# Out projection, way up and way down of a two-block transformer on one core: buffers laid over freed bytes, and the order of work at the borders of the stages

## The chip, the core and the metric

The kernel runs on one core of a Trainium2 chip. The core has TensorE (matmuls and transposes into PSUM; PE in the profile, its weight loads PEld), VectorE (DVE), ScalarE (ACT), GpSimd (POOL) and SyncE (SP), which here issues every transfer, one after the other. The metric is device time in microseconds; lower is better. The times are whole executions; the profile is one further execution.

## What is computed

Two transformer blocks over 1024 rows of 1024 float32 numbers, one after the other. Cut to the parts around the change:

```python
# first block
x = x + mix @ w_out                       # mix: attention, conv and pool branches
h2 = rms_norm(x, norm2_g)
up = causal_depthwise_conv(h2 @ w_up, ffn_dw_w)      # 5632 columns, width 3
gate, val = split(up)
x = x + (silu(gate) * val) @ w_down       # 2816 rows
# second block
h = rmsnorm(x, pre_mix_w)                 # feeds q, k, v and the gates
x = x + rmsnorm(merged @ w_out, post_mix_w)
h = rmsnorm(x, pre_ffn_w)
f = (silu(h @ w_gate) * (h @ w_up)) @ w_down
x = x + rmsnorm(f, post_ffn_w)
```

## The kernel before

Every float32 operand of a matmul is split into a high part (a cast on ScalarE) and a low part (raw minus high, on GpSimd or VectorE in turn, `lo_of`), and a product of two operands is three matmuls (`mm3`, L117): high by high, high by low, low by high. A matmul has 128 x 128 weights and mostly 512 columns.

The stages run one after the other: `mix1` (norm, projections, attention and branches), `out1` (first out projection), `ffn` with the convolution, then a norm and transposes, `mix2`, `merge2`, `out2` (second out projection, then its norm and the sum with x), and `ffn` without convolution, which ends with the last norm. `ffn` has three parts.

- `ffn_prelude` normalises the eight row blocks of 128 rows (Square on ScalarE, L734; the inverse root on GpSimd, L155 and L157; the scaling on VectorE, L736), forms sums and differences of their quarters, and transposes seven operands T1 to T7 of 512 x 512 (`put`, L719 to L726: four transposes, a cast on ScalarE, the low part on VectorE). T1 and T2 come from rows 0 to 3 as they are; the other five need rows 4 to 7 as well.
- `ffn_up` multiplies by a scheme of seven products in place of eight (of the kind of Strassen's). For each of 22 channel blocks it loads two weight tiles, forms four sums, splits them (`split`, L778) and runs seven products of 12 matmuls, 84 in all. Partial results are copied from PSUM (`snap`, L837), summed into G and V (`add`, L850), sent through convolution and SiLU (`finish`, L809), and the operands of the way down go to DRAM (gD).
- `ffn_down` runs 11 pairs of channel blocks in groups of 2, 3, 3 and 3: it loads operands from gD and from w_down (`load`, L890), splits them (L931, L932), runs seven products per group and adds them to the accumulator rows `acc` (`to`, L905; L912), which in the first block are loaded from x1D first (L888).

On each engine a scheduler of the tile framework fixes the order of the instructions at build time; the code's order and the tiles' lifetimes steer it. A tile that takes bytes of an earlier one waits for that one's last reader. Transfers stand in one queue on SyncE: one that waits holds up those behind it. `ffn` opens its pools when the stage before has closed its own:

```python
            with self.pool("fpre") as fp:
                self.ffn_prelude(rows, keep, g, T, fp, ps)
            close_rows()
            with self.pool("fst", side="right") as st:
                self.ffn_up(T, fw, st, ps, Wg, cg, Wu, cu, conv, gD)
```

## Time and profile before

| what | value |
|---|---|
| time, median of 3 runs | 2932.63 us (2928.97 to 2937.85) |
| the profiled execution, its time | 2919.26 us |
| its span | 2917.4 us |
| mean granted clock of TensorE in it | 0.963 |
| TensorE busy | 2711.6 us |
| VectorE, ScalarE, GpSimd busy | 1802.7, 1210.0, 909.9 us |
| transfers | 375.10 MB, 129 GB/s on average |

Busy is time in which an engine has an instruction in work. A count of matmuls in a stretch, beside the count in a stretch of the same matmuls without waits, tells how much of the stretch was lost; a waits view tells which engine's result ended each wait. A few records can be missing, so a count is good to about one per cent.

### The profile page before, as it was taken

To read this page: it belongs to the slowest core of one execution; us is meant where nothing else is said; L and a number is where in the kernel's file an instruction comes from. 1 tells how busy PE (TensorE), PEld (TensorE's weight loads), DVE (VectorE), ACT (ScalarE), POOL (GpSimd) and SP (SyncE) were. 2 spreads that over 40 slices of the span, in tenths; PEclk is the share of its full clock that TensorE was granted. 3 is DMA by queue.
4 is the path that set the end of the run, shared out by engine and by line. 5 is a ranking of instruction groups with operands and counts; after the bars stand their busy time and mean duration, and the time that the engine had idled before them with its cause. 6 is when DMAs were issued, how large, how long until landed. Compare 5 with 4: busy or idle time off the path is not lost. (4 is left out here: it accounts for less than half of the span.)

```text
span 2917.4 us, 37487 instructions
## 1 busy us (share of the span) xinstructions
PE 2711.6 (93%) x13686; PEld 2269.2 (78%) x13686; DVE 1802.7 (62%) x2832; ACT 1210.0 (41%) x1951; POOL 909.9 (31%) x686
## 2 busy tenths in 40 slices
PE   7999889699999889989999999999986999998997
PEld 7799678477777767878889988887875888886776
DVE  4697653678788796735666533444436555556877
ACT  4344561344444433334445444444313433334333
POOL 3256331122222244521211254323511212123445
PEclk9999999699999989989999999999996999999999
DMA  5444451122322383065664395415430333336532
GB/s 175 122 136 127 144 177 67 52 80 98 109 94 87 130 312 129 26 204 161 173 171 121 111 224 131 138 60 182 137 130 15 100 102 101 102 106 230 169 122 87
DMA packets 318145, 375.10 MB, mean 129 GB/s; under 512 B 42692, under 2 KB 215168, under 8 KB 317448
## 3 DMA queue, kind: packets, MB, share of 16 engines
q1 hardware_dynamic: 317960, 372.70, 41.2%
q8 instruction: 108, 1.77, 0.2%
q14 instruction: 77, 0.63, 0.1%
HBM read 257.01 MB, written 115.61 MB: 128 GB/s over the span
## 5 line engine op out<-in xcount | busy, mean ns | idle before, releaser
L138 POOL TENSOR_TENSOR wl<-wr,wh 128x1024 fp32r<-128x1024 f32 x73 | 184.8, 2534 | 343.4 <-ACT wh L137 303.8
L759 POOL TENSOR_TENSOR lo<-x,hi 128x1024 fp32r<-128x1024 f32 x77 | 205.7, 2684 | 270.5 <-ACT hi L931 269.1
L931 ACT CAST hi<-x 128x1024 fp32r<-128x1024 f32 x154 | 153.1, 1052 | 274.1 <-PE x L117 123.4
L759 POOL TENSOR_TENSOR wl<-ws,wh 128x512 fp32r<-128x512 f32 x88 | 115.6, 1315 | 469.8 <-ACT wh L781 383.5
L117 PE MATMUL mm<-hTh,wh 128*128 128x512 f32 x608 | 244.2, 402 | 4.1 <-ACT gs L1125 4.1
L117 PE MATMUL mm<-hTh,wl 128*128 128x512 f32 x608 | 241.6, 397 | 0.0
L309 ACT ACTIVATE t<-t,mx 128x640 f32<-128x640 f32 (+3 forms) x192 | 173.3, 903 | 163.4 <-DVE mx L305 154.6
L117 PE MATMUL mm<-hTl,wh 128*128 128x512 f32 x608 | 241.1, 396 | 0.0
L117 PE MATMUL mm<-wh,hTh 128*128 128x256 f32 (+1 forms) x752 | 228.9, 305 | 3.8 <-ACT hTh L184 1.9
L117 PE MATMUL mm<-wh,hTl 128*128 128x256 f32 (+1 forms) x752 | 228.4, 304 | 1.4 <-DVE hTl L185 1.4
L117 PE MATMUL mm<-wl,hTh 128*128 128x256 f32 (+1 forms) x752 | 227.9, 303 | 0.3 <-POOL wl L138 0.3
L781 ACT CAST wh<-ws 128x512 fp32r<-128x512 f32 x176 | 109.2, 623 | 263.1 <-PE x L117 145.0
L357 DVE TENSOR_TENSOR pl<-tr,ph 128x512 fp32r<-128x512 f32 (+2 forms) x160 | 100.6, 633 | 126.2 <-ACT ph L356 48.6
L326 POOL TENSOR_SCALAR t<-t,rs 128x640 f32<-128x640 f32 (+7 forms) x128 | 106.7, 840 | 204.3 <-DVE rs L325 179.8
L117 PE MATMUL x<-hi 128*128 128x512 f32 x352 | 139.7, 405 | 31.4 <-DVE f L912 17.1
L759 POOL TENSOR_TENSOR wl<-wr,wh 128x1024 fp32r<-128x1024 f32 (+1 forms) x44 | 94.0, 2136 | 200.5 <-ACT wh L781 160.1
L117 PEld LDWEIGHTS mm<-wh,hTh 128*128 128x128 f32 x752 | 144.9, 193 | 11.6 <-ACT hTh L184 2.9
L117 PEld LDWEIGHTS mm<-wh,hTl 128*128 128x128 f32 x752 | 145.0, 193 | 7.1 <-DVE hTl L185 1.6
L117 PEld LDWEIGHTS mm<-wl,hTh 128*128 128x128 f32 x752 | 145.1, 193 | 6.3 <-POOL wl L138 0.9
L117 PE MATMUL x<-lo,hi 128*128 128x512 f32 x352 | 140.6, 400 | 4.2 <-DVE lo L759 2.9
L117 PE MATMUL x<-hi,lo 128*128 128x512 f32 x352 | 140.1, 398 | 0.0
L117 PEld LDWEIGHTS mm<-hTh,wh 128*128 128x128 f32 x608 | 116.2, 191 | 29.2 <-ACT gs L1125 5.2
(334 smaller groups left out, 7764.6 us busy)
## 6 DMA issues: line engine op xcount, KB each, us to landing
x<-gD SPq DMA_DIRECT2D x154, 256.0 KB, 4.6
wr<-in_w_up_dram SPq DMA_DIRECT2D x66, 512.0 KB, 3.7
wr<-in_w_in_dram SPq DMA_DIRECT2D x50, 512.0 KB, 7.6
gD<-gs SPq DMA_DIRECT2D x98, 256.0 KB, 2.2
gD<-gp SPq DMA_DIRECT2D x88, 256.0 KB, 2.1
x<-in_w_down_dram SPq DMA_DIRECT2D x66, 256.0 KB, 3.7
wr<-in_w_gate_dram SPq DMA_DIRECT2D x22, 512.0 KB, 3.8
wr<-in_w_out_dram SPq DMA_DIRECT2D x16, 512.0 KB, 5.3
```

Of the source, the lines that this page charges most:

```text
L117: self.nc.tensor.matmul(out, lhsT, rhs, start=start, stop=stop, **kw)
L138: g = (lo_engine or nc.gpsimd).tensor_tensor(out=lo, in0=raw[:, :n], in1=hi.bitcast(F32), op=ALU.subtract)
L309: nc.scalar.activation(out=t[:, :nb * P], in_=t[:, :nb * P], func=AF.Exp, scale=-1.0, bias=m, accum_out=s)
L326: nc.gpsimd.tensor_scalar(out=t[:, :nb * P], in0=t[:, :nb * P], scalar1=r, scalar2=1.0, op0=ALU.mult, op1=ALU.mult)
L357: nc.vector.tensor_tensor(out=pl[:, :w], in0=tr[:, :w], in1=ph[:, :w].bitcast(F32), op=ALU.subtract)
L759: return eng.tensor_tensor(out=lo, in0=raw, in1=hi.bitcast(F32), op=ALU.subtract)
L781: nc.scalar.copy(out=hi, in_=raw)
L931: nc.scalar.copy(out=hi, in_=raw)
```

## The change

What a stage keeps in memory is laid over bytes that the stage before frees step by step, and work of a stage is written into the code of the stage before.

- `ffn_prelude` is gone. Its norms and sums are done per row (`pre_row`) from inside `out1` and `out2` (`done`), in place; T1 and T2 are transposed there. The other five operands are transposed in `ffn_up`, between products 1 and 2 of channels 0 and 1. In `out1` rows 0 to 3, and not 4 to 7, get most of their second half early.

```diff
+DOWN = (1, 5, 6, 7, 4, 3, 2)
+LATE = (6, 5, 7, 4, 3)
+NX = 21
 CAUSAL = [(0, i + 1) for i in range(NB)]
 HELD = 3
...
-        for i in range(4, NB):
+        for i in range(4):
             part(i, 1, w1[:6])
         self.split_T(self.mixD[3], mT, 3)
+        gB, jk = (self.wpool.tile([P, D], F32, tag="wr", name=self.n("wr"), bufs=2) for _ in range(2))
+        nc.sync.dma_start(out=gB, in_=I["norm2_g"][0].partition_broadcast(P))
         for i in range(NB):
             part(i, 0, w0)
-            part(i, 1, w1 if i < 4 else w1[6:])
+            part(i, 1, w1[6:] if i < 4 else w1)
+            done(i, gB, jk)
...
+    def pre_row(self, i, rows, keep, gB, jk, T, pool, ps):
+
+        nc = self.nc
+        x = rows[i][:, :D]
+        if keep is not None:
+            nc.sync.dma_start(out=keep[i * P:(i + 1) * P, :], in_=x)
+        self.norm_rows(x, x, jk, gB)
+        k0, k1 = x[:, :512], x[:, 512:]
+        if i < 4:
+            self.put(T, 1, i, k0, ps)
+            self.put(T, 2, i, k1, ps)
+            return
+        j = i - 4
+        b11, b21 = rows[j][:, :512], rows[j][:, 512:D]
+        t2 = pool.tile([P, 512], F32, tag="t2", name=self.n("t2"))
+        nc.vector.tensor_tensor(out=b11, in0=k0, in1=b11, op=ALU.subtract)
+        nc.vector.tensor_tensor(out=t2, in0=k1, in1=b11, op=ALU.subtract)
+        nc.vector.tensor_tensor(out=k0, in0=k1, in1=k0, op=ALU.subtract)
+        nc.vector.tensor_tensor(out=b21, in0=b21, in1=t2, op=ALU.subtract)
+        self.sums[j] = {6: t2, 5: b11, 7: k0, 4: b21, 3: k1}
```

- `ffn_up`: high and low parts of all weight splits share eight slots; there are four splits per channel (three of 1024 columns, one of 512) where there were six. G, V, the snapshots and the results lie in the eight rows R of the stage before. Products 1 to 7 come in another order, and the last channel in one of its own.

```diff
+        G, V, b_ = R[0], R[1], R[2][:, :S]
+        t1, t2, t3, s1, s2, s4 = (R[i][:, o:o + 512] for i, o in ((3, 0), (3, 512), (4, 0), (4, 512), (7, 0), (7, 512)))
+        gp = [R[5][:, :S], R[6][:, :S]]
+        snaps = {1: t1, 2: t2, 3: t3}
+
+        def split(raw, w):
+            hi, lo = (fw.tile([P, 1024], F32R, tag="w", name=self.n("w"), bufs=8)[:, :w] for _ in range(2))
+            nc.scalar.copy(out=hi, in_=raw)
+            self.lo_of(lo, raw, hi)
+            return [(hi[:, o:o + 512], lo[:, o:o + 512]) for o in range(0, w, 512)]
...
+            A = chans[c] = {}
+            A[1], A[2] = split(r[0].rearrange("p h x -> p (h x)"), 1024)
+            raws[c] = r
...
-            A[7], = split(s3, 512)
+            u, v = (fw.tile([P, 2, 512], F32, tag="ws", name=self.n("ws"), bufs=2) for _ in range(2))
+            nc.vector.tensor_tensor(out=u[:, 0], in0=a21, in1=a22, op=ALU.add)
+            nc.vector.tensor_tensor(out=u[:, 1], in0=u[:, 0], in1=a11, op=ALU.subtract)
+            A[5], A[6] = split(u.rearrange("p h x -> p (h x)"), 1024)
+            nc.vector.tensor_tensor(out=v[:, 0], in0=a11, in1=a21, op=ALU.subtract)
+            nc.vector.tensor_tensor(out=v[:, 1], in0=a12, in1=u[:, 1], op=ALU.subtract)
+            A[7], A[3] = split(v.rearrange("p h x -> p (h x)"), 1024)
             A[4], = split(a22, 512)
...
+        puts(2)
+        begin(0)
+        product(0, 1, "x", True)
+        puts(2)
+        product(0, 2, "z", True)
+        weights_b(0)
+        puts(4)
+        begin(1)
+        product(1, 1, "x", True)
+        puts(6)
+        product(1, 2, "z", True)
+        puts(6)
...
+        for c in range(2, NF):
+            last = c == NF - 1
+            weights_a(c)
+            weights_b(c)
+            p1(c)
+            p4(c - 1)
+            if last:
+                p3(c - 1)
+            product(c, 6, "x", False)
+            if not last:
+                p3(c - 1)
+            snap(c, 2)
+            if last:
+                product(c, 2, "z", True)
+                g11(c)
+                p7(c)
+                product(c, 5, "y", True)
+            else:
+                product(c, 5, "y", True)
+                product(c, 2, "z", True)
+                g11(c)
+                p7(c)
+            v22(c)
+        p4(NF - 1)
+        p3(NF - 1)
```

- `ffn_down`: operands lie in 21 slots over the weights and T3, T4, and in the eight rows; `load` takes a list of pairs and loads product by product; the accumulator's loads are written behind the first group's; PSUM is one tag of eight banks.

```diff
+        def operand():
+            n = count[0] % (NX + NB)
+            count[0] += 1
+            if n < NX:
+                return fx.tile([P, 2, 512], F32, tag="x", name=self.n("x"), bufs=NX)
+            return self.right(n - NX)[:, :S].rearrange("p (a b) -> p a b", a=2)
+
+        def load(ps_):
+
+            X = {p: {} for p in ps_}
...
+                for p in ps_:
+                    X[p][i] = operand()
+            for i in (1, 5, 6, 7, 4, 3, 2):
+                for p in ps_:
+                    r0, r1 = Wd[2 * p * P:(2 * p + 1) * P], Wd[(2 * p + 1) * P:(2 * p + 2) * P]
+                    nc.sync.dma_start(out=X[p][i][:, 0], in_=gD[p, i - 1])
+                    src = {1: r0[:, :512], 5: r0[:, 512:], 3: r1[:, 512:], 2: r1[:, :512]}.get(i)
+                    if src is not None:
+                        nc.sync.dma_start(out=X[p][i][:, 1], in_=src)
...
+        loaded = load(groups[0])
+        if not fresh:
+            for i in range(NB):
+                nc.sync.dma_start(out=acc[i], in_=keep[i * P:(i + 1) * P, :])
...
+            x = [ps.tile([P, 512], F32, tag="b", name=self.n("x")) for _ in range(4)]
...
+                    hi, lo = (fh.tile([P, 1024], F32R, tag="hl", name=self.n("hl"), bufs=12) for _ in range(2))
```

- The norm before `mix2` is done in place on `acc` as soon as a row is stored (`stored`); only the transposes stay behind. `out2` computes half rows ahead and holds them in PSUM, loads all eight rows of x2D at its start, and normalises each row twice as it ends.

```diff
+    def stored(i, acc, spare):
+        if "g" not in held:
+            held["g"], held["j"] = spare(), spare()
+            nc.sync.dma_start(out=held["g"], in_=I["pre_mix_w_2"][0].partition_broadcast(P))
+        nc.sync.dma_start(out=x2D[i * P:(i + 1) * P, :], in_=acc[i])
+        net.norm_rows(acc[i], acc[i], held["j"], held["g"])
...
+        for i in range(NB):
+            nc.sync.dma_start(out=rows[i][:, :D], in_=xD[i * P:(i + 1) * P, :])
+        with self.pool("pq", 1) as pq:
+            gp = self.bcast_row(I["post_mix_w_2"][0], pq)
+            gB = self.bcast_row(I["pre_ffn_w_2"][0], pq, tag="gf")
...
+            def first(i, dh, ws):
+                tag, bufs = ("pv", 1) if i == 7 else ("sc", 3)
+                half[i] = (dh, self.proj(i, mT, ws, ps.tile([P, 512], F32, tag=tag, name=self.n(tag), bufs=bufs)))
+
+            def second(i, ws):
+                dh, pa = half.pop(i)
...
+                for d, p in ((dh, pa), (1 - dh, pt)):
+                    ds = slice(d * 512, (d + 1) * 512)
+                    nc.vector.scalar_tensor_tensor(out=o[:, ds], in0=p, scalar=r, in1=gp[:, ds], op0=ALU.mult, op1=ALU.mult)
+                x = rows[i][:, :D]
+                nc.vector.tensor_tensor(out=x, in0=o, in1=x, op=ALU.add)
                 nc.sync.dma_start(out=yD[i * P:(i + 1) * P, :], in_=x)
+                return o
...
+                for i in range(3):
+                    first(i, 1, w1)
+                for i in range(4):
+                    o = second(i, w0)
+                    done(i, gB, o, False)
+                    if i == 0:
+                        first(3, 1, w1)
+                for i in range(4, NB):
+                    first(i, 0, w0)
+            early()
+            for i in range(4):
+                done(i, gB, None, True)
+            for i in range(4, NB):
+                o = second(i, w1)
+                done(i, gB, o, True)
```

Matmuls and transposes are as many as before. The order on the engines at three places follows. First TensorE, at the end of out projection 1 (mm); tr are transposes of operand blocks, x and z product banks, x_1041 and so on are rows of the stage, t a sum of theirs. Before:

```order
L117 MATMUL mm_5330<-KH_5042,hTh_4791 128x512
L117 MATMUL mm_5330<-cB_5043,hTh_4791 128x512
L117 MATMUL mm_5330<-KH_5042,hTl_4793 128x512
L722 MATMUL tr_5380<-ident,x_1041_4782 128x128 x4
L722 MATMUL tr_5387<-ident,x_1041_4782 128x128 x4
...
L722 MATMUL tr_5449<-ident,x_1044_4785 128x128 x4
L722 MATMUL tr_5456<-ident,x_1044_4785 128x128 x4
L117 MATMUL x_5700<-T1h_5352,wh_5668 128x512
L722 MATMUL tr_5472<-ident,x_1045_4786 128x128 x4
```

After:

```order
L118 MATMUL mm_5456<-KH_5056,hB_4806 128x512
L118 MATMUL mm_5456<-cB_5057,hB_4806 128x512
L118 MATMUL mm_5456<-KH_5056,hB_4807 128x512
L722 MATMUL tr_5535<-ident,t_1136_5349 128x128 x4
L722 MATMUL tr_5542<-ident,t_1142_5396 128x128 x4
L118 MATMUL x_5550<-T1h_4797,w_5513 128x512
L118 MATMUL x_5550<-T1l_4798,w_5513 128x512
L118 MATMUL z_5551<-T2h_4799,w_5513 128x512
```

Before, eight blocks of transposes follow the last mm, and products mix with the other 20 blocks later; after, two blocks of product 6's operand follow it, and then products 1 and 2 of channels 0 and 1, 48 matmuls.

Second SyncE at the end of way up 1 (gD out, wr weights, f the accumulator rows, x operands of the way down). Before:

```order
L835 DMA gD_5342<-gs_9029 128x512
L897 DMA x_9102<-in_w_down_dram 128x512
L895 DMA x_9159<-gD_5342 128x512
L897 DMA x_9159<-in_w_down_dram 128x512
...
L895 DMA x_9223<-gD_5342 128x512
L895 DMA x_9224<-gD_5342 128x512
L888 DMA f_9048<-x1D 128x1024
L888 DMA f_9049<-x1D 128x1024
```

After:

```order
L870 DMA gD_5499<-r_1046_4791 128x512
L992 DMA f_8606<-x1D 128x1024
L992 DMA f_8607<-x1D 128x1024
...
L992 DMA f_8613<-x1D 128x1024
L870 DMA gD_5499<-r_1047_4792 128x512 x2
L870 DMA gD_5499<-r_1045_4790 128x512
...
L870 DMA gD_5499<-r_1046_4791 128x512
L965 DMA x_8623<-gD_5499 128x512
L968 DMA x_8623<-in_w_down_dram 128x512
```

The loads of f stood behind the loads of the first operands, and now stand ahead of the last stores to gD and of all operands.

Third SyncE at the start of out projection 2 (wr output weights, xr and r the rows of x2D, gB broadcast gains). Before:

```order
L134 DMA wr_19424<-in_w_out_dram 128x2x512
L134 DMA wr_19430<-in_w_out_dram 128x2x512
L134 DMA wr_19451<-in_w_out_dram 128x2x512
L162 DMA gB_19475<-in_post_mix_w_dram 128x1024
L1210 DMA xr_19717<-x2D 128x1024
L134 DMA wr_19457<-in_w_out_dram 128x2x512
L1210 DMA xr_19756<-x2D 128x1024
```

After:

```order
L135 DMA wr_18967<-in_w_out_dram 128x2x512
L135 DMA wr_19003<-in_w_out_dram 128x2x512
L1270 DMA r_3877_18977<-x2D 128x1024
L1270 DMA r_3878_18978<-x2D 128x1024
...
L1270 DMA r_3884_18984<-x2D 128x1024
L163 DMA gB_18996<-in_post_mix_w_dram 128x1024
L163 DMA gB_18998<-in_pre_ffn_w_dram 128x1024
L135 DMA wr_19009<-in_w_out_dram 128x2x512
L135 DMA wr_19015<-in_w_out_dram 128x2x512
L135 DMA wr_19021<-in_w_out_dram 128x2x512
```

The row loads, which came one by one between the weights and the stores, now stand together ahead of the last three weight tiles.

## Rows read from the trace of the kernel before

**Rows 1.** The page, part 1: busy us, share, instructions.

```profile
PE 2711.6 (93%) x13686; PEld 2269.2 (78%) x13686; DVE 1802.7 (62%) x2832; ACT 1210.0 (41%) x1951; POOL 909.9 (31%) x686
```

**Rows 2.** Windows, TensorE alone: stretch, width, busy (matmuls), granted clock, DMA share, GB/s.

```profile
490.00:600.00 110.00, 82.72 (x347) 0.78 0.21 67
600.00:1000.00 400.00, 387.94 (x1666) 1.00 0.29 95
1000.00:1050.00 50.00, 31.66 (x105) 0.76 0.86 319
1050.00:1250.00 200.00, 196.56 (x865) 1.00 0.38 130
...
2165.00:2275.00 110.00, 76.84 (x324) 0.77 0.23 70
2275.00:2650.00 375.00, 375.00 (x1656) 1.00 0.31 101
2650.00:2705.00 55.00, 44.20 (x165) 0.88 0.89 318
2705.00:2900.00 195.00, 185.42 (x800) 0.99 0.32 103
```

**Rows 3.** Waits of TensorE, 490 to 600: us in total, times, longest.

```profile
PE tr L722 <- DVE x L736: 8.4, 3, 5.0
```

**Rows 4.** Waits of TensorE, 600 to 1000.

```profile
PE x L117 <- POOL wl L759: 8.1, 10, 1.7
```

**Rows 5.** Waits of TensorE, 1000 to 1050.

```profile
PE x L117 <- DVE f L912: 9.2, 1, 9.2
PE x L117 <- ACT hi L931: 5.1, 2, 3.2
```

**Rows 6.** Waits of TensorE, 1250 to 1285.

```profile
PE tr L181 <- DVE hTl L185: 7.5, 4, 4.6
```

**Rows 7.** Waits of TensorE, 2165 to 2275.

```profile
PE tr L722 <- DVE x L736: 19.4, 4, 14.1
```

**Rows 8.** Waits of TensorE, 2650 to 2705.

```profile
PE x L117 <- ACT hi L931: 8.7, 2, 5.9
```

**Rows 9.** Waits of TensorE, 2705 to 2900.

```profile
PE y L117 <- DVE lo L759: 5.0, 2, 4.4
```

**Rows 10.** Groups by shape, 490 to 600: count | busy us, mean ns | idle before.

```profile
L736 DVE SCALAR_TENSOR_TENSOR x<-x,rr,gB 128x1024 f32<-128x1024 f32 x8 | 13.1, 1665 | 4.1 <-DMA gB<-in_norm_g_dram 2.8 <-POOL rr L157 1.3
...
L734 ACT ACTIVATE jk<-x 128x1024 bf16<-128x1024 f32 x6 | 6.4, 1060 | 11.3 <-DVE x L679 11.3
...
L157 POOL TENSOR_TENSOR rr<-rv,mhalf 128x1 f32<-128x1 f32 x6 | 3.6, 603 | 0.5
...
L155 POOL TENSOR_SCALAR rv<-ms 128x1 f32<-128x1 f32 x6 | 2.0, 334 | 43.6 <-ACT jk L734 43.5
```

**Rows 11.** Groups by shape, 600 to 1000.

```profile
L759 POOL TENSOR_TENSOR wl<-wr,wh 128x1024 fp32r<-128x1024 f32 x20 | 57.1, 2854 | 74.4 <-ACT wh L781 71.2 <-DVE wl L759 3.1
...
L775 DVE TENSOR_TENSOR ws<-wr,wr 128x512 f32<-128x512 f32 x19 | 48.2, 2537 | 0.0
...
L781 ACT CAST wh<-wr 128x1024 fp32r<-128x1024 f32 x19 | 19.9, 1047 | 3.9 <-PE z L117 3.9
```

**Rows 12.** Groups by shape of VectorE, 2275 to 2650.

```profile
L759 DVE TENSOR_TENSOR wl<-wr,wh 128x1024 fp32r<-128x1024 f32 x19 | 23.1, 1216 | 0.0
...
L775 DVE TENSOR_TENSOR ws<-wr,wr 128x512 f32<-128x512 f32 x19 | 13.1, 692 | 22.2 <-POOL wl L759 22.2
```

**Rows 13.** Transfers: issues, KB each, median us from issue to landing.

```profile
x<-gD SPq DMA_DIRECT2D x154, 256.0 KB, 4.6
...
x1D<-x SPq DMA_DIRECT2D x8, 512.0 KB, 2.6
...
f<-x1D SPq DMA_DIRECT2D x8, 512.0 KB, 7.8
...
x2D<-f SPq DMA_DIRECT2D x8, 512.0 KB, 4.0
```

433 lines of the change are left out of this document (189 added, 244 removed).

## The prediction

> **What bounds the kernel now.** I read the busy shares first: TensorE is busy 93% of the span [rows 1], so only time in which it waits can be won, unless work is taken away, and no matmul is. Next I cut the span into stages by the count of matmuls [rows 2]. In the second way up TensorE never waits: 1656 matmuls in 375 us, 0.2264 us each at the granted clock 1.00. Width minus count times 0.2264 is what a stage loses:
>
> - out projection 1 into way up 1 (490 to 600): 110 - 78.6 = 31.4
> - way up 1 (600 to 1000): 400 - 377.2 = 22.8
> - way up 1 into way down 1: 50 - 23.8 = 26.2
> - way down 1: 4.2
> - out projection 2 into way up 2: 110 - 73.4 = 36.6
> - way up 2: 0
> - way up 2 into way down 2: 55 - 37.4 = 17.6
> - way down 2: 13.9
>
> These eight make 152.7. Way down 1 into the second block isn't counted that way, since its matmuls have other widths; the waits give at least 7.5 [rows 6], and I take 10. So some 163 us are idle or at a granted clock under 1 (0.76 to 0.88 at the borders [rows 2]), and a border's loss holds both. I then asked at each border which wait ends last. Transposes wait for the normalised rows [rows 3, 7]; the first matmuls of way down 1 wait for the accumulator rows [rows 5]; those of way down 2 wait for ScalarE's casts [rows 8]. That points at work done after the last matmul of the stage before, and that is what the change moves.
>
> **The change part by part.** I sum against the profiled execution (2919.26 us, its span 2917.4) and carry the difference to the median, 2932.63, which lies 13.4 us higher.
>
> *Out projection 1 into way up 1.* Before, eight scalings and 28 transposed blocks follow the last out-projection matmul. Now a row is normalised as soon as its sums are done, T1 and T2 are transposed between rows, and products 1 and 2 of channels 0 and 1 (48 matmuls, 10.9 us) lie among the 20 blocks of the other five operands. One row's chain is Square 1.06, two GpSimd steps of some 0.9 together, and the scaling at 1.67 [rows 10]: 3.6 us. Rows 0 to 3 give TensorE 12 matmuls and 8 transposes, 4.5 us each; rows 4 to 7 give 30 matmuls, 6.8 us. VectorE needs two adds, the scaling and two low parts in the first case, 4 x 0.69 + 1.67 = 4.4, and two adds, the scaling and four differences in the second, 6 x 0.69 + 1.67 = 5.8 (0.69 per 512 columns as in [rows 12]). So it fits, the first case barely. What is added: the scaling now writes in place, so it must wait for the store of the same row, 2.6 us from issue to landing [rows 13]. The adds of the next row are queued behind it on VectorE, and TensorE's two banks wait for those. Cost: 3 of the first rows by at most 2.6 - 1.06 - 0.9 = 0.6, 2 us. Then ScalarE has the cast of T1's last block queued behind the Square of row 7 (the last matmul, add 0.69, Square 1.06, and what stands ahead): 4 us. The 20 blocks then come in pairs of banks, each cast and low part 0.6 + 0.7 beside 0.9 of transposes; 12 of the blocks have products beside them, the others give up 0.4: 3 us. With 3 for the clock this leaves 12 of 31.4: **19 won** (12 if the blocks aren't hidden, 24 if only the cast is late).
>
> *Way up 1.* Four splits per channel in place of six, eight shared slots, G, V and snapshots in the freed rows. The first split of the next channel takes the slot that product 4 frees. That product ends 12 matmuls before the block's end, and the new block has 4 matmuls that need only the high part: 16 x 0.2264 = 3.6 us for a cast of 1.05 and a GpSimd split of 2.85 [rows 11], 3.9 us. So 0.3, with semaphores 0.5, in each of 20 blocks: 10 us, and I allow 3.5 for the first channels. Before, it was 22.8, of which the same split made 8.1 [rows 4]. **9 won** (0 if the split is held up as now, 18 if it starts early).
>
> The slots also bring twice a 1024-column split on GpSimd per channel, not one and two of 512. The trace shows what that does to VectorE: the sum ws<-wr,wr, which runs beside it, takes 2.54 us [rows 11], and 0.69 in the second way up, where no such split runs [rows 12]. The Trainium skill, SBUF — State Buffer, section Who interferes with whom, says that a VectorE instruction with two SBUF inputs and a GpSimd instruction that reads SBUF exclude one another, and that the second to issue is blocked until the first ends; the trace agrees. By that rule the added split costs VectorE 1.85 us more per channel, 37 over 20 channels: none of the sum while VectorE has slack, up to 37 less if it has none.
>
> *Way up 1 into way down 1.* The accumulator's loads (7.8 us to land [rows 13]) move from behind the first operands' loads to before the last stores of way up 1, so the 9.2 wait goes [rows 5]. Next late are the casts, 5.1 now [rows 5]. From the eighth operand on, loads lie over split slots of channel 21 and start after its product 3: 4.6 to land, cast 1.05, split 2.85, 8.5 us [rows 11, 13]; they are covered by three products of two pairs, 72 matmuls or 16.3 us. Not covered is VectorE's own queue, which has the last channel's convolution ahead of the first splits: an add, five 1024-column steps and a ScalarE step between, 0.69 + 5 x 1.22 + 1.05 = 8 us [rows 11, 12]; with the casts and the clock, 14 remain. **12 won** (6 to 20).
>
> *Way down 1 and its end.* Eight banks under one tag: **2 won**. The norm before the second block moves under the last products; its in-place scaling waits for the store of the same row, 4.0 us [rows 13], and the low parts of the first transposes stand behind four scalings. I put 8 where 10 were: **2 won** (-3 to 5).
>
> *Out projection 2 into way up 2.* The largest loss; of 36.6 the transposes' wait for scaled rows makes 19.4 [rows 7]. Products come under it as in block 1, but two things stay. In rows 4 to 7 VectorE needs six 512-column steps, an add and a scaling of 1024, 6 x 0.69 + 2 x 1.22 = 6.6 us [rows 12], beside 24 matmuls, 5.4: 1.2 x 4 = 5 late, and the last row's chain with its differences, partly under products, 6; with 5 for the clock 16. New is SyncE's queue: eight row loads (4 MB) and two broadcasts (1 MB) now stand ahead of the last three pairs of output weights. At the 318 GB/s of the busiest borders [rows 2] that is 16 us, and the cover, three half rows, is 72 matmuls, 16.3 us, less the weights' own load, cast and split: 8 late (0 to 10). So 24 of 36.6: **12 won** (4 to 24).
>
> *Way up 2 into way down 2, way down 2, way up 2.* The casts' wait, 8.7 [rows 8], gets the slots earlier, and the last channel's product order frees T6 and T7 first: 9 of 17.6 left, **8 won** (3 to 13). In way down 2 the wait for low parts (5.0 [rows 9]) goes, as pairs' operands arrive in product order: **7 won** (0 to 10). In way up 2 VectorE does the first split in 1.22 [rows 12], and 1.05 + 1.22 is under 3.6: 0 (-5 to 0).
>
> The sum: 19 + 9 + 12 + 2 + 2 + 12 + 8 + 7 = **71 us**. 2919.3 - 71 = 2848 profiled; from the median 2932.6 - 71 = **2862**.
>
> **The rivals.** *Borders close almost wholly.* If the in-order waits above are hidden, the clock stays at 1.00 and each border leaves 4 to 6 us; with 10 in the ways up and 8 in the ways down some 50 of 163 are left: 113 won, **2820**. For it speaks that each chain is shorter than its cover; against it, that the covers are within 1 us of it. *Queues swallow the gain.* The stores that in-place scalings wait for and the weights behind row loads cost as much at both out projections as the norms did: 19 and 12 become 7 and 0; the first split stalls way up 1 as today, 9 becomes 0; the other 31 stay but for 3: about 35 won, **2898**. *Slower: the first split of each channel comes late.* One mechanism, in both ways up: the split that may start only when product 4 has freed its slot is queued behind the channel's other work on its engine. If it ends d after the slot is free, a block loses d - 3.6, and 40 blocks (20 in each way) lose 40 x (d - 3.6) + 3.5, against 22.8 now. The other terms win 62, so the kernel is slower by 9 us from d = 6.0, 2.4 per block. With the other 1024-column split ahead on GpSimd in way up 1, d is 1.05 + 2 x 2.85 = 6.75 [rows 11]; with the channel's product, four sums and the split on VectorE in way up 2, 1.05 + 2 x 1.22 + 4 x 0.69 = 6.25 [rows 12]. At 6.5 on average 40 x 2.9 + 3.5 - 22.8 - 62 = 35 are lost: **2968**. Against it: now TensorE waits 8.1 for that split in 400 us, never over 1.7 at a time [rows 4], and in way up 2 never. *Nothing moves.* The tile scheduler may have overlapped what can be overlapped: **2933**. Against it stand the borders themselves.
>
> **How the numbers follow.** Forecast 0.53, borders close 0.17, queues 0.20, slower 0.06, nothing 0.04. The range has the two outer cases' centres, 2820 and 2898, and 7 us beyond them, about what the runs of the kernel before lie apart (2928.97 to 2937.85): 2813 to 2905; the slower case and no change are left out. About 0.3%, 9 us, can be told from no change, so faster is 0.53 + 0.17 + 0.20 = 0.90, same 0.04, slower 0.06.
>
> **What would show it.** Right: the matmul count of the 110 us around each out projection's end rises from 347 and 324 to some 430 and 380; the f L912 wait at way down 1's start is gone; waits of way up 1 are for GpSimd's first split, 0.3 to 0.5 each. Wrong: out projection 2 waits for weights by more than 10 us, way up 2 counts fewer than 1640 in 375 us, or VectorE's scalings wait for stores while TensorE stands.

## The result and the profile after

The changed kernel takes 2890.26 us (median of 4 runs, 2889.24 to 2897.29) beside 2930.93 us for the kernel before on the same chip (4 runs, 2928.97 to 2937.85): ratio 0.9862, 95% interval 0.9839 to 0.9885. By medians 40.7 us are won, where 71 were forecast. The profiled executions lie nearer together, 2919.26 and 2889.56 us, 29.7 apart, since the profiled execution of before was shorter than its timed runs; the stretches below are of these two.

The page of the changed kernel, part 1 (busy us, share, instructions), answers to [rows 1]; the rows under it are its windows, at stretches that correspond to those of [rows 2] (width; busy and count of TensorE, its weight loads, VectorE, ScalarE, GpSimd; granted clock; DMA share; GB/s).

```profile
PE 2696.8 (93%) x13686; PEld 2264.4 (78%) x13686; DVE 1800.6 (62%) x2738; ACT 1193.0 (41%) x1863; POOL 934.4 (32%) x642
```

```profile
490.00:600.00 110.00, 97.15 (x453) 77.71 (x452) 75.30 (x99) 42.28 (x66) 20.51 (x20) 0.95 0.23 74
600.00:980.00 380.00, 377.63 (x1646) 307.41 (x1645) 300.00 (x311) 182.44 (x217) 118.49 (x38) 1.00 0.34 109
980.00:1040.00 60.00, 45.68 (x162) 35.24 (x161) 57.37 (x58) 20.78 (x21) 22.30 (x9) 0.83 0.90 329
...
2160.00:2270.00 110.00, 92.62 (x412) 73.48 (x410) 73.84 (x95) 44.08 (x74) 30.01 (x24) 0.91 0.27 83
...
2635.00:2695.00 60.00, 43.66 (x171) 33.70 (x170) 47.15 (x42) 27.02 (x36) 26.58 (x9) 0.89 0.91 322
```

The out projections' ends hold 453 and 412 matmuls in 110 us (347 and 324 before), but the 60 us behind each way up hold 162 and 171, which at 0.2264 us each is 37 and 39 us of work. That is where the forecast's gain is missing. The ends of the stages say the same. They are read from TensorE's matmuls by tile (start of the last one of a stage, or of the first; us from the span's start):

| | out 1 ends | way up 1 ends | way down 1 ends | mixing 2 starts | out 2 ends | way up 2 ends | way down 2 ends | span |
|-|-|-|-|-|-|-|-|-|
| before | 510.2 | 1009.8 | 1249.5 | 1267.1 | 2177.7 | 2660.0 | 2899.5 | 2917.4 |
| after | 527.5 | 981.2 | 1224.2 | 1238.5 | 2172.5 | 2636.8 | 2869.6 | 2887.2 |

So up to the end of way up 1 the change wins 28.6 us, way down 1 loses 3.3 (239.7 to 243.0 us from the way up's last matmul to its own), the step into mixing 2 wins 3.3, mixing 2 to the end of way up 2 loses 5.4 (1392.9 to 1398.3), way down 2 wins 6.7 (239.5 to 232.8), the tail 0.3. The border between the step and mixing 2 has moved: the step has 40 transposes in the trace of before and 20 now, the others stand behind mixing 2's first matmul. From way down 1's end to mixing 2's last product with the attention values it took 722.6 us and takes 724.3.

TensorE's waits in the changed kernel, stretch by stage (us in total, times, longest). First 465 to 600, then 600 to 980, where nothing else waits, in answer to [rows 3, 4]:

```profile
PE mm L118 <- ACT hA L127: 8.2, 1, 8.2
PE x L118 <- ACT w L778: 2.9, 1, 2.9
```

```profile
PE x L118 <- ACT r L821: 2.4, 2, 1.7
```

Behind way up 1 (970 to 1060, [rows 5] before), in out projection 2 (2070 to 2165) and at its end (2165 to 2275, [rows 7]):

```profile
PE x L118 <- DVE f L982: 4.2, 1, 4.2
PE y L118 <- ACT hl L1004: 3.5, 1, 3.5
PE x L118 <- ACT hl L1004: 3.2, 1, 3.2
```

```profile
PE mm L118 <- ACT woh L138: 6.0, 1, 6.0
PE sc L118 <- POOL wl L139: 2.2, 1, 2.2
```

```profile
PE tr L722 <- DVE T6l L726: 6.5, 2, 5.9
PE tr L722 <- DVE t L744: 4.4, 2, 3.3
```

Behind way up 2 (2630 to 2695, [rows 8]) and in way down 2 (2695 to 2870, [rows 9]):

```profile
PE y L118 <- ACT hl L1004: 9.2, 1, 9.2
PE x L118 <- ACT hl L1004: 2.8, 1, 2.8
```

```profile
PE x L118 <- DVE f L982: 0.8, 2, 0.6
```

The waits for normalised rows, 8.4 and 19.4 before, are gone but for 4.4 us at the second border, for differences of the last row (`t`), as is the wait for GpSimd's split in way up 1 (8.1). New are 8.2 us for the last head's result ahead of out projection 1, 6.0 for cast weights in out projection 2, and 9.2 for the cast of way down 2's product 5 (`y`, the second product of a group to run).

### The profile page after: what moved, and what is told of

Read it like the earlier page. It is cut to its first block, busy times and chain, and to the rows that moved or that the text cites. A ratio compares the mean times of both kernels' runs of the same rounds, so it can differ in the third digit from the quotient of the medians.

```text
span 2887.2 us, 37070 instructions
## 1 busy us (share of the span) xinstructions
PE 2696.8 (93%) x13686; PEld 2264.4 (78%) x13686; DVE 1800.6 (62%) x2738; ACT 1193.0 (41%) x1863; POOL 934.4 (32%) x642
## 4 chain that ended last, share of the span: by engine, by line
PE 44%; DMA 5%; DVE 5%; issue 3%; POOL 3%; ACT 1%; SPq 1%; POOLq 0%; DVEq 0%; ACTq 0%
PE mm L118 14%; PE x L118 12%; PE y L118 6%; PE sc L118 4%; PE pv L118 3%; PE z L118 2%; PE tr L359 1%; PE tr L1073 1%; DVE hl L766 1%; DVE f L982 1%; DVE x L972 1%; POOL hl L766 1%; DMA wr<-yD 1%; POOL g L1239 1%; DMA x<-in_w_down_dram 1%
## 5 line engine op out<-in xcount | busy, mean ns | idle before, releaser
L766 POOL TENSOR_TENSOR hl<-x,hl 128x1024 fp32r<-128x1024 f32 x61 | 167.1, 2748 | 222.7 <-ACT hl L1004 202.4
L118 PE MATMUL x<-hl,hl 128*128 128x512 f32 x704 | 219.4, 397 | 5.9 <-DVE hl L766 4.4
L766 POOL TENSOR_TENSOR w<-ws,w 128x1024 fp32r<-128x1024 f32 x44 | 137.4, 3124 | 247.2 <-ACT w L778 247.2
L118 PE MATMUL mm<-hA,wh 128*128 128x512 f32 x608 | 197.1, 399 | 4.4 <-ACT gs L1199 4.4
L118 PE MATMUL mm<-hB,wh 128*128 128x512 f32 x608 | 197.2, 398 | 1.7 <-ACT gs L1199 1.7
L118 PE MATMUL y<-hl,hl 128*128 128x512 f32 x528 | 163.3, 396 | 5.3 <-DVE hl L766 4.0
L118 PE MATMUL mm<-wh,hB 128*128 128x256 f32 (+1 forms) x752 | 162.8, 305 | 1.4 <-ACT hB L180 1.4
L118 PEld LDWEIGHTS x<-hl,hl 128*128 128x128 f32 x704 | 134.7, 192 | 36.5 <-DVE hl L766 6.7
L118 PE MATMUL mm<-wh,hA 128*128 128x256 f32 (+1 forms) x704 | 150.0, 301 | 10.6 <-ACT hA L127 8.2
L118 PE MATMUL x<-hl 128*128 128x512 f32 x352 | 137.5, 398 | 16.1 <-DVE f L982 10.1
```

The lines of the kernel that those rows point to most:

```text
L118: self.nc.tensor.matmul(out, lhsT, rhs, start=start, stop=stop, **kw)
L766: return eng.tensor_tensor(out=lo, in0=raw, in1=hi.bitcast(F32), op=ALU.subtract)
```

## Experiments

Each kernel is the changed one with the edit shown. Most ran once, so the stretch that the edit touches is read and not the total: where the code is the same, way down 1 measured 240.2 to 244.7 us in five kernels and way down 2 232.5 to 234.7. The second block's mixing, from its first matmul to its last product with the attention values, takes 707.8 to 711.5 us in all thirteen kernels with the change.

**Weights ahead of the rows in out projection 2.**

```diff
-        for i in range(NB):
+        for i in range(2):
             nc.sync.dma_start(out=rows[i][:, :D], in_=xD[i * P:(i + 1) * P, :])
...
                 for k in (0, 2, 4, 6):
                     w0 += self.pair(W, k, 0, pool=pp, th="woh", tl="wol", bufs=4)
+                gB = self.bcast_row(I["pre_ffn_w_2"][0], pq, tag="gf")
+                for i in range(2, NB):
+                    nc.sync.dma_start(out=rows[i][:, :D], in_=xD[i * P:(i + 1) * P, :])
```

> Second out projection of the changed kernel: six of its eight row loads and one broadcast (3.5 MB) are written behind the loads of the four pairs of second-half weights; nothing else is changed. In the changed kernel the last three pairs are issued at 2085.6 to 2100, behind the row loads at 2072.3 to 2085.6, and TensorE idles 6.0 and 0.8 us for them and runs ten microseconds at half the clock. Theory (the queue's order costs it): the wait for the weights' cast falls from 6.0 to under 2 us, the stretch at a granted clock of 0.5 goes, and the second way up's last product ends 9 to 13 us earlier against the end of the gated sum. Rival (the transfers' rate is the limit, whatever the order): the scheduler needs the rows soon after, VectorE's sums then wait for them and TensorE's banks for VectorE: 0 to 3 us.

2878.25 us. From the start of mixing 2 to the end of out projection 2: 925.5 us instead of 934.0; from the last product with the values to the end of way up 2 681.1 instead of 688.3. The wait for the cast is gone, 1.4 and 2.2 us for GpSimd's low parts are left. Of the two rows below, the first is the changed kernel, the second this one, which is some 4 us ahead there: 33 matmuls at a granted clock of 0.85, so partly at the lower level (1.2 GHz), became 59 at 1.00 (2.4 GHz).

```profile
2085.00:2100.00 15.00, 8.15 (x33) 5.91 (x31) 0.00 (x0) 2.09 (x2) 2.52 (x2) 0.85 0.77 302
```

```profile
2085.00:2100.00 15.00, 13.60 (x59) 10.56 (x58) 0.00 (x0) 2.14 (x3) 5.83 (x3) 1.00 0.55 216
```

So the weights behind four MB of rows cost 7 to 8 us, just under the 9 to 13 that were expected of the edit.

**More early halves, or others, in out projection 1.**

```diff
-        for i in range(4):
+        for i in range(NB):
             part(i, 1, w1[:6])
...
-            part(i, 1, w1[6:] if i < 4 else w1)
+            part(i, 1, w1[6:])
```

> First out projection of the changed kernel: all eight rows, in place of rows 0 to 3, get the first 18 matmuls of their second half before the last attention head's result is read back; four more additions on VectorE, the matmuls are the same. Theory (too little independent work is left for the 8.2 us in which the last head's result is stored, loaded and cast): the wait of 8.2 us goes, with the 8 us at half clock behind it, and the last product of way up 1 ends 6 to 11 us earlier. Rival (the work is only moved: what fills the gap is missing under the norms of rows 4 to 7, which then have 12 matmuls each): the last out-projection matmul comes earlier by 8 to 12 us, but the last product of way up 1 by under 3.

> First out projection of the changed kernel: rows 4 to 7 get 18 matmuls early, as in the kernel before, and not rows 0 to 3; the rest as in the changed kernel. Theory (the early rows are finished soon in the changed order, which leaves nothing for the 8.2 us): with rows 4 to 7 early some 20 more matmuls stand behind the last attention product, the wait falls to 3 to 5 us; but rows 0 to 3 are normalised later, and rows 4 to 7 have 12 matmuls each under which their norms lie, so the last product of way up 1 ends within 5 us of where it ends now. Rival (which rows come early doesn't matter there, the result simply lands late): wait 7 to 9 us as now.

All eight rows: 2876.22 us; the 8.2 wait is gone, and from the last head's product with the values to the end of way up 1 it takes 495.0 us instead of 507.2. It leaves more for products' weights (all_rows_early, waits from 465 to 600):

```profile
PE x L118 <- POOL w L766: 5.2, 1, 5.2
PE x L118 <- ACT w L778: 4.1, 1, 4.1
```

Four rows, but rows 4 to 7 (`range(4, NB)`): 2890.95 us and 510.2 us, and 7.5 of the wait stays. So it isn't which rows are early but how many matmuls are left behind the last head. With four early rows, whichever they are, the scheduler has put all their halves ahead of it: TensorE runs no matmul between the last head's last product and the wait, in which that head's result is stored, loaded and cast. With all rows early it runs 49 there.

**Block b12 in a place of its own.** Each pair has four blocks b11, b12, b21, b22 of w_down; the way down forms differences of them. The change overwrites b12 by b12 - b11, so b22 - b12 has to come first, and product 5 waits for b22, the ninth of a pair's eleven loads.

```diff
-                        nc.sync.dma_start(out=X[p][i][:, 1], in_=src)
+                        nc.sync.dma_start(out=X[p][6 if i == 5 else i][:, 1], in_=src)
...
-                for out, x, y in ((t3, b22, b12), (b12, b12, b11), (t2, b22, b12), (t4, b21, t2)):
+                for out, x, y in ((t1, t2, b11), (t3, b22, t2), (t2, b22, t1), (t4, b21, t2)):
```

> Ways down of the changed kernel: the block b12 of the down weights is loaded into the place of product 6's difference and product 5's difference b12 - b11 is written to its own place first; before, b12 was overwritten in place, so that product 7's difference b22 - b12 had to come first, and with it the load of b22, the tenth or later of a group. As many loads and subtractions as before. Theory (that added dependence holds product 5 up): TensorE's wait for the cast of product 5 in the second way down (9.2 us) falls to under 3, the 3.5 us one in the first way down goes as well, and the stretch from the last product of the way up to the last of the way down gets 6 to 10 us shorter in block 2 and 2 to 6 in block 1. Rival (the rate of the operand loads, 380 to 400 GB/s for 40 us, is the limit): product 5 starts earlier, product 6 or 7 waits instead, under 3 us in all.

2882.71 us. Way down 1 238.2 us instead of 243.0; way down 2 237.1 instead of 232.8. Product 5's wait is gone, and in its place TensorE waits in way down 2 for product 6's cast (2.6 us) and further on for a low part (4.4). The dependence was real, but not the bound in block 2, which took longer than in any kernel without the edit.

**The blocked store.** At the way up's end SyncE comes to the first store of the last channel pair, and it waits there for VectorE's product of gate and value for the last channel but one (L861): 10.0 us in block 1, until 979.5, and 14.2 in block 2. The way down's loads stand behind it. In SyncE's waits of the changed kernel (940 to 1250) these are the stores' waits (the longest, 10.5, is that of the pair before), and under them SyncE's timeline at the end of way up 1: seven stores, the last of them the one that waits, then the loads.

```profile
SPq L870 <- DVE r L861: 22.6, 4, 10.5
```

```profile
961.68 18.14 SPq L870 DMA_DIRECT2D gD<-r  x7
979.91 0.38 SPq L965 DMA_DIRECT2D x<-gD  x1
980.34 0.44 SPq L968 DMA_DIRECT2D x<-in_w_down_dram  x1
980.89 0.36 SPq L965 DMA_DIRECT2D x<-gD  x1
```

```diff
-                for i, t in ((1, a11), (2, a12), (3, s4), (4, a22), (5, s1), (6, s2), (7, a21)):
-                    nc.sync.dma_start(out=gD[c // 2, i - 1], in_=t)
+                parts = ((2, a12), (3, s4), (4, a22), (5, s1), (6, s2), (7, a21), (1, a11))
+                for i, t in parts:
+                    d = nc.sync.dma_start(out=gD[c // 2, i - 1], in_=t)
+                    if i == 1 and c == NF - 1:
+                        self.tc.add_manual_dep(d.ins, mark.ins.name, NOSYNC, reason="late")
+                    mark = d
```

> In the last channel pair of each way up, the store of the block that waits for VectorE last goes out behind the six others, so SyncE comes to the way down's operand loads about 10 to 19 us sooner; nothing else is changed. Theory, that one blocked store holds the loads: the first operand load of block 1 is issued near 967 on the scale of the changed kernel's trace instead of 979.9, and the stretch from the last matmul of the way up to the last of the way down falls from 243.0 us to 232 to 237 in block 1 and from 232.8 us to 222 to 228 in block 2; the time is 2870 to 2880. Rival, that the operand buffers or the 390 GB/s at which these loads land set the pace: the loads are issued sooner, but the stretches stay within 3 us of 243.0 and 232.8, and the time within 5 us of 2890.

> The same late store, and the block b12 of the way down's features in a place of its own, so that the fifth product no longer waits for b22's load. Theory, that the late loads and the overwritten block are two causes of the waits after the way up: both stretches come out below those of the late store alone, by 3 to 6 us in block 1. Rival, that with loads issued early the dependence costs nothing: within 2 us of the late store alone, in either direction, in both blocks.

The same views with the late store:

```profile
SPq L871 <- DVE r L861: 15.1, 3, 10.5
SPq L969 <- PE x L118: 8.9, 1, 8.9
```

```profile
960.51 4.66 SPq L871 DMA_DIRECT2D gD<-r  x6
966.74 0.32 SPq L969 DMA_DIRECT2D x<-gD  x1
968.12 0.33 SPq L972 DMA_DIRECT2D x<-in_w_down_dram  x1
977.46 0.32 SPq L969 DMA_DIRECT2D x<-gD  x1
```

The first operand's two loads start 13.2 us sooner in block 1 and 20.0 in block 2 (2607.7 for 2627.7), and nothing comes of it: 241.4 and 234.6 us, at the scatter, total 2884.36. For behind them stands the next wait: the second operand's place is still held by a product of the way up, 8.9 us in block 1 and 19.3 in block 2. Measured from the way up's last matmul, the second operand's load starts 2.2 us sooner in block 1 and no sooner in block 2. With b12 apart as well: 238.1 and 232.7, 2880.69. So my theory, formed when I saw that wait on SyncE, fell: the store wasn't what held the loads. What loads that all start 13 to 20 us sooner would bring, no run shows.

**Sums behind the transposes.**

```diff
         product(0, 2, "z", True)
-        weights_b(0)
         puts(4)
...
         puts(6)
+        weights_b(0)
         close_sums()
```

> In the way up, the weight block sums of the second channel pair (VectorE and ScalarE work) are emitted behind the last group of transposes instead of ahead of it; nothing else is changed. Theory, that VectorE's queue at the border from the out projection to the way up holds the transposes' copies behind those sums: the stretch from the last matmul of out projection 2 to the last of way up 2 falls from 464.3 us by 3 to 8, and TensorE's waits for copies of transposed rows between 2170 and 2250 fall from some 18 us to under 10. Rival, that the norm of the last row and the copies themselves are the chain: those waits stay within 3 us, and the sums, now later, add a wait for weights of 2 to 6 us in the second pair, so that the stretch is 464 to 470.

2884.62 us; from out projection 2's end to way up 2's 461.4 us instead of 464.3, and the two transposes' waits 5.6 and 4.4 instead of 6.5 and 4.4. Kernels that leave this stretch alone show 461.4 as well as 464.3, so nothing is shown to be won; what holds those transposes stays open.

**What holds way down: order of arrival or VectorE.** VectorE's row for the 60 us behind way up 1 had been there all along. Windows of before (behind each way up), then of the changed kernel:

```profile
1009.80:1069.80 60.00, 42.33 (x153) 32.56 (x152) 55.92 (x57) 18.22 (x19) 20.47 (x8) 0.80 1.01 373
2660.00:2720.00 60.00, 48.71 (x185) 36.83 (x184) 51.29 (x50) 28.85 (x37) 27.84 (x10) 0.89 0.91 322
```

```profile
981.20:1041.20 60.00, 45.68 (x162) 35.31 (x161) 58.12 (x59) 20.06 (x20) 23.50 (x9) 0.83 0.91 329
2636.80:2696.80 60.00, 43.66 (x171) 33.69 (x171) 48.95 (x43) 27.49 (x36) 27.57 (x9) 0.89 0.91 321
```

The third busy time (with its count) is VectorE's: 55.92 of 60 us before, 58.12 after. Two edits tell its own work from the dependence on late blocks. In the first the four subtractions of a pair become additions of the same size inside the operand's own tile (same work, no foreign blocks); in the second ScalarE copies for products 6, 7 and 4, and VectorE does nothing (both leave out the differences, so neither computes the transformer):

```diff
             for p in ps_:
-                b11, b12, b22, b21, t2, t3, t4 = (X[p][i][:, 1] for i in (1, 5, 3, 2, 6, 7, 4))
-                for out, x, y in ((t3, b22, b12), (b12, b12, b11), (t2, b22, b12), (t4, b21, t2)):
-                    nc.vector.tensor_tensor(out=out, in0=x, in1=y, op=ALU.subtract)
+                for i, src in ((5, 1), (6, 0), (7, 0), (4, 0)):
+                    t = X[p][i]
+                    nc.vector.tensor_tensor(out=t[:, 1], in0=t[:, 0], in1=t[:, src], op=ALU.add)
```

```diff
-            for p in ps_:
-                b11, b12, b22, b21, t2, t3, t4 = (X[p][i][:, 1] for i in (1, 5, 3, 2, 6, 7, 4))
-                for out, x, y in ((t3, b22, b12), (b12, b12, b11), (t2, b22, b12), (t4, b21, t2)):
-                    nc.vector.tensor_tensor(out=out, in0=x, in1=y, op=ALU.subtract)
             return X
...
                 for p in grp:
+                    if i in (6, 7, 4):
+                        nc.scalar.copy(out=loaded[p][i][:, 1], in_=loaded[p][i][:, 0])
```

> On the kernel with the late store, the four VectorE subtractions of each pair of weight blocks in the way down become four VectorE additions of the same size whose inputs lie in the operand's own tile, so that products 5, 6, 7 and 4 no longer wait for blocks that are loaded for other products (the output is not the reference's). VectorE's work stays as it is. Theory, that with the loads issued early the time after the way up goes to the order in which blocks arrive: the stretches from the way up's last matmul to the way down's last (241.4 and 234.6 us with the late store alone) fall to 230 to 235 in block 1 and 222 to 228 in block 2. Rival, that VectorE's own time sets the pace (busy 58 of 60 us behind the way up in block 1 of the changed kernel): block 1 stays at 238 to 242, and block 2, where VectorE is busy 49 of 60 us, falls by at most 4.

> On the kernel with the late store, the same four subtractions are left out; for products 6, 7 and 4 ScalarE copies the operand's first half into its second, for product 5 nothing is done (the output is not the reference's). So the dependence on other blocks is gone as in the run with additions in the own tile, and some 25 us of VectorE's time in the first 75 us behind the way up of block 1 with it. Theory, that VectorE sets the pace in block 1: its stretch falls to 222 to 230 us, well under that of the run with additions, and block 2's by 3 to 8 us more than there. Rival, that loads at 390 GB/s set it: both stretches within 3 us of the run with additions.

> The same leaving out of the four subtractions on the changed kernel itself, with its stores in their old order (the output is not the reference's). Theory, that VectorE is the pace and the store only delays what VectorE could not take up anyway: the late store is worth more once VectorE is free, so this run's stretches come out 5 to 12 us above those of the run with late store and copies in block 1, and 8 to 15 in block 2. Rival, that loads 13 to 20 us earlier are worth nothing here either: within 3 us of it.

| way down, us from the way up's last matmul | block 1 | block 2 | time |
|-|-|-|-|
| changed kernel | 243.0 | 232.8 | 2889.56 |
| late store | 241.4 | 234.6 | 2884.36 |
| late store, additions in the own tile | 237.6 | 222.7 | 2871.16 |
| late store, copies on ScalarE | 222.8 | 216.5 | 2849.58 |
| stores as changed, copies on ScalarE | 222.8 | 214.4 | 2843.33 |

Windows behind way up 1 and 2 with the copies and the stores as changed:

```profile
979.60:1039.60 60.00, 51.40 (x207) 40.04 (x207) 53.66 (x51) 32.47 (x42) 25.28 (x11) 0.94 0.97 349
2609.80:2669.80 60.00, 57.00 (x244) 46.31 (x243) 36.52 (x38) 42.10 (x59) 30.52 (x12) 0.97 0.98 356
```

Against the late store alone, the dependence is worth 3.8 us in block 1, no more than the scatter there, and VectorE's subtractions 14.8; in block 2 it is 11.9 and 6.2. Each comes from one run, and "VectorE's subtractions" are their time and their place in VectorE's queue together, which no run tells apart. Matmuls in the first 60 us go from 162 to 207 and from 171 to 244. The rate of the loads, the rival of the copies' run, is not what bounds the changed kernel there: the same 60 us move 349 and 356 GB/s with the copies, where they moved 329 and 321. The last two kernels differ in the store's place alone, and their ways down agree within 2.1 us, so the store costs nothing with VectorE free either.

**Versions that beat both kernels.** Eight early rows, weights ahead of rows and the late store; then the same with b12 apart:

> Three edits in one: all eight rows' early halves in out projection 1, out projection 2's weight loads ahead of six of its row loads, and the late store. Theory, that the three lie in separate stretches and add: 12 us and 8 us from the runs of the single edits, and 8 to 20 us if the late store holds the loads, which gives 2850 to 2862 where the changed kernel has 2890; without a gain of the late store, 2867 to 2872. Rival, that a gain in one stage is given back in the next, as the two block 2 stretches showed for the fifth product: 2872 to 2880.

> The three edits of the earlier combined run (all rows' early halves, weights ahead of row loads, late store) and b12 in a place of its own. By the single runs the last edit took 3.3 us off block 1's stretch and 1.9 us off block 2's where the store was late, which gives 2863 to 2867 beside 2869.75 for the three; the rival, that its waits move on to the next products, gives 2868 to 2872.

The first takes 2869.75 us (4 runs, 2867.99 to 2871.93) beside 2923.48 for the kernel before on its chip: ratio 0.9816, interval 0.9800 to 0.9833. That is the expectation for a late store without a gain. The second takes 2863.62 us (4 runs, 2857.89 to 2874.50) beside 2923.67: ratio 0.9802, interval 0.9763 to 0.9841. Its way down 1 takes 234.0 us where the first has 241.3, its way down 2 233.1 where that has 233.5. The two intervals overlap, so that the second is the faster isn't settled. The first's lies under the changed kernel's (0.9839 to 0.9885); the second's, whose runs lie further apart, just reaches it, with the lower median.

## Why the prediction was right and wrong

Direction and range held; the sum, 71, was 30 us too high by medians and 41 by the profiled executions. The term that failed most is way down 1 with its start, 12 + 2 forecast. Point by point, in the prediction's steps:

*Out projection 1 and way up 1: 19 + 9 forecast, 28.6 measured*, the sum right by two errors, so by luck. (It is good to some 5 us: in kernels with the same code up to there way up 1 ends at 977 to 981 us, and the changed kernel is the last of them.) Way up 1 was to keep a stall of 0.5 us in each of 20 blocks for GpSimd's first split; no such wait is in the trace. The stretch loses 380 - 1646 x 0.2264 = 7.3 us where I left 13.5, some 15 won instead of 9. The border wins the rest, some 13 instead of 19: the step "eight scalings and 28 blocks" was right, and what took its place, the 8.2 us for the last head, has no term in the sum. TensorE's clock falls with it: from 475 to 490 it has 20 matmuls at 0.66, between its levels of 1.2 and 2.4 GHz.

```profile
475.00:490.00 15.00, 7.14 (x20) 5.29 (x21) 4.83 (x7) 2.29 (x4) 0.75 (x2) 0.66 0.34 114
```

All eight rows early takes it away and brings 12 us. The store waits that I priced at 2 us are there, in VectorE's waits from 475 to 540:

```profile
DVE r L188 <- DMA x1D<-r: 6.3, 3, 2.3
```

TensorE waits 1.4 us for an addition behind the first of them, so the price was about right, and the rival that enlarged it doesn't hold. The slower rival, a first split that comes late, is ruled out: TensorE waits for no such split in either way up. (Its own working gives 15 us lost at d = 6.0; the 9 belong to d = 5.86.)

The Trainium skill's rule that I weighed (SBUF — State Buffer, Who interferes with whom: a VectorE instruction with two SBUF inputs and a GpSimd instruction that reads SBUF exclude one another) would take up to 37 us if VectorE had no slack. Here it is busy 300.0 of 380 us and TensorE waits 2.4, so the price stays off the path in way up 1. Nor does it fall where I put it: the sum `ws<-wr,wr` takes 0.68 us in the changed kernel, and the product of gate and value, at 1.29 before, takes 2.71 (means from 600 to 1000 and 600 to 980).

*Way up 1 into way down 1: 12 + 2 forecast, -3.3 measured.* This is the step that failed most, and it failed in its reading of the 9.2 us wait for `f` L912 [rows 5]: I took it for the accumulators' loads. But this is VectorE's row for these additions in the kernel before, in the 60 us behind way up 1 (1009.8 to 1069.8), with its idle time ahead of them:

```profile
L912 DVE TENSOR_TENSOR f<-x,f 128x512 f32<-128x512 f32 x13 | 8.7, 685 | 2.6 <-PE x L117 2.2 <-DMA f<-x1D 0.3
```

It stood idle 0.3 us for those loads. During the 9.2 us (1035.5 to 1044.7) it was busy without a break with low parts and subtractions, and the first addition followed on them without a gap. The loads, issued from 1037.0 on, were no more than the next limit. So with VectorE's queue in that order, earlier loads alone could not take the wait away. It went to 4.2, with VectorE idle 0.1 us ahead of the additions (last section). Then "not covered is VectorE's own queue ... 8 us; with the casts and the clock, 14 remain" counted the last channel's convolution and left out the subtractions of weight blocks and the accumulations, which keep VectorE at 58 of 60 us. What remained is 243.0 - 924 x 0.2264 = 34 us, not 14 at the start and 2 further on. I had costed what TensorE waits for last, and hadn't read how full the other engines are in that stretch; before's 55.92 of 60 said that a removed wait would only let VectorE be late a little sooner.

*Way down 1 into mixing 2: 2 forecast, 3.3 measured* up to mixing 2's first matmul, but 20 transposes have moved behind it. Up to the last product with the values it is 1.7 lost (722.6 to 724.3), where the kernels with the change scatter from 722.3 to 726.3. So no gain is shown.

*Out projection 2, way up 2: 12 + 0 forecast, -5.4 measured* from mixing 2's first matmul, 5.0 of it in mixing 2, for the moved transposes above all. From the last product with the values it took 687.9 us and takes 688.3, so -0.4. The two terms that I named were sized well: 110 - 412 x 0.2264 = 16.7 left at the border (16 forecast), and 8 for weights behind rows (7 to 8 by the run). What has no term is out projection 2 ahead of its end, which loses some 15 us more than before, 7 beyond those 8 (from the last product with the values: 205.6 us for 864 matmuls before, 224.0 for 864 and 32 transposes now). These are TensorE's waits there, before (1972 to 2177) and after (1948.5 to 2172):

```profile
PE mm L117 <- ACT gs L1125: 5.6, 4, 3.5
PE mm L117 <- POOL wl L138: 0.3, 1, 0.3
```

```profile
PE mm L118 <- ACT gs L1199: 7.6, 4, 3.5
PE mm L118 <- ACT woh L138: 6.0, 1, 6.0
PE sc L118 <- POOL wl L139: 2.2, 1, 2.2
PE mm L118 <- POOL wol L139: 0.8, 1, 0.8
```

That is 10 to 11 us more of waits, the weights' casts and low parts above all, and from 2093 to 2108 the granted clock is 0.66. Then come 4 to 5 us in way up 2, which I held to be without loss: products with T1 and T2 are slower there (last section). One price in the prediction was wrong at both out projections: a transpose of 128x128 counts there like a matmul of 512 columns, 0.2264 us, but takes 0.109 at the full clock. With 112 of them a border lost 13 us more before than the sum has it.

*Way up 2 into way down 2: 8 + 7 forecast, 6.7 measured.* The wait in way down 2 went, as said. "As pairs' operands arrive in product order" was wrong: the overwritten b12 ties product 5 to b22, and the 8.7 us for ScalarE's casts came back as 9.2 for that product. Breaking all ties brings 11.9 us, VectorE's work 6.2 more.

*The rivals.* 2898, queues swallow the gain, is nearest in time, but of its three mechanisms only weights behind rows costs TensorE what it says. "Borders close", 2820, failed at the ways down: what TensorE has to do there doesn't cover VectorE's work. That VectorE bounds the way down's start wasn't among the rivals and should have been.

*The signs.* Of those for being right one shows: 453 and 412 matmuls, more than the 430 and 380. Of those for being wrong, out projection 2 waits 9.0 us for weights, under the 10 named, but way up 2 counts 1628 in 375 us (2252 to 2627), fewer than 1640, and a scaling does wait for a store while TensorE stands, 1.4 us.

## What to carry to other kernels

Before a removed wait is booked as a gain, read what the engine that ended it was doing (here VectorE stood idle 0.3 us for the loads that were blamed), and the busy time of every engine in that stretch: where one of them is busy 56 of 60 us, look there for what is late next, whichever row the waits show. An intermediate written over an input that others still need puts the order of loads into the dependence; here it cost more in the block where VectorE had slack. And behind one wait on a queue the next may stand: with the store out of the way, one operand was loaded 13 to 20 us sooner, and the second waited for its place.

## What the runs showed of the hardware

VectorE's groups in the changed kernel's 60 us behind way up 1 (981.2 to 1041.2; count | busy us, mean ns | idle before):

```profile
L972 DVE TENSOR_TENSOR x<-x,x 128x512 f32<-128x512 f32 x14 | 15.7, 1128 | 1.6 <-DMA x<-in_w_down_dram 1.5
L766 DVE TENSOR_TENSOR hl<-x,hl 128x1024 fp32r<-128x1024 f32 x7 | 12.8, 1840 | 0.0
L982 DVE TENSOR_TENSOR f<-x,f 128x512 f32<-128x512 f32 x16 | 10.5, 680 | 0.1
```

Beside GpSimd's splits a subtraction of 512 columns with both inputs in SBUF takes 1128 ns on average; an addition of the same size with one input in PSUM takes 680. The average hides two kinds: most subtractions take 674 to 693 ns, six take 1.8 to 2.9 us, and each of the six ends 544 to 551 ns after a GpSimd split that began before it. Additions that overlap such a split take 674 to 692 ns. In way up 2 of the kernel before, with no GpSimd split of that size beside it, a sum of weight blocks took 692 [rows 12]. That agrees with the exclusion that the Trainium skill states (SBUF — State Buffer, Who interferes with whom), and the rows say which work on VectorE pays for GpSimd's: the sums of weight blocks, not the accumulations.

Unexpected, and not explained: in way up 2 matmuls whose moving operand is T1 or T2 take 397 ns in the changed kernel, the others 389 to 391; before, all took 389. (In way up 1 they take 397 too.) The rows are from 2280 to 2580:

```profile
L118 PE MATMUL z<-T2h,w 128*128 128x512 f32 x127 | 42.6, 397 | 0.0
...
L118 PE MATMUL x<-T1h,w 128*128 128x512 f32 x123 | 41.3, 397 | 0.0
...
L118 PE MATMUL x<-T4h,w 128*128 128x512 f32 x120 | 39.4, 389 | 0.0
```

40 us hold 176 matmuls instead of 178, which over the 1848 of a way up is 4.7 us. These two are the operands that the change moved ahead into a place of their own; in the compiled program it starts 32 bytes past a multiple of 64, where the other five start at a multiple. Whether that is the cause wasn't tried.
